# Layer norm's column sums taken from four square tiles in PSUM, and two operand splits moved beside an earlier projection

## The chip, the core and the metric

The kernel runs on one core of a Trainium2 chip. The core has five engines with queues of their own: TensorE (PE, with its weight loads shown as PEld), VectorE (DVE), ScalarE (ACT), GpSimd (POOL) and SyncE (SP), which issues DMA transfers. Each works through its own list of instructions in order and waits on semaphores for the others. The metric is the device time of one execution in microseconds (us); the median of three runs counts.

## What is computed

Two transformer-like blocks act on one sequence of 512 positions and 1024 channels, in FP32. The change touches the first block's mixer alone:

```python
def hybrid_mixer(h, w_in, b_f, conv_w, conv_b, conv_ln_g, conv_ln_b, w_o):
    proj = h @ w_in                     # q, k, v, f_logit, conv_val, conv_gate
    ...
    attn = fox_attention(q, k, v, log_f)             # 8 heads of 64, causal
    u = conv_val * jax.nn.sigmoid(conv_gate)
    u = causal_depthwise_conv(u, conv_w, conv_b)     # 512 channels, 31 taps
    u = jax.nn.silu(layer_norm(u, conv_ln_g, conv_ln_b))
    return jnp.concatenate([attn, u], axis=-1) @ w_o
```

`layer_norm` takes mean and variance over the 512 channels of a position. Behind the mixer stand a gated residual, a SwiGLU network, and the second block (a state-space mixer and a stick-breaking attention).

## The kernel before

**Tiles and precision.** The sequence is four blocks of 128 positions, the channels are blocks of 128 partitions. Projections are split products: each FP32 operand is a rounded part (hi) and its rest (lo), and `mm3` issues three matmuls (L328 hi by hi, L329, L330), each 128 rows by 512 columns, in a fast FP32 format. An ordinary FP32 matmul stands in the trace as two records, since it takes two passes.

**Where the weights come from.** SP loads weights into four raw buffers (L247). ACT rounds a raw tile (L269, `whi`) and DVE or POOL takes the rest (L273, `wlo`). Between them DVE adds up rows of other weight matrices for the modulation vectors (L503, L505).

**Layer norm over channels.** The convolution's result `yc` has channels on partitions: four tiles of 128 channels by 512 positions. A sum over channels is therefore a sum over partitions, which PE does: `colsum` (L487) multiplies a tile by a column of ones, in four pieces of 32 columns for each block of 128 positions, so that the result has one column. The steps are:

- `centre`: PE sums the total of the four tiles (L1027), DVE subtracts the mean from each (L1029);
- `square(ct)`: ACT squares tile `ct` (L1033), and POOL adds the squares, 0 to 1 and 2 to 3 (L1035) and then both sums (L1037);
- `factor`: PE takes the column sums of that one tile (16 matmuls, L487), DVE works out the inverse root in twelve small steps (L1045, L594 to L601);
- `row` and `scale`: PE spreads the factors over the partitions (L609), ACT copies them (L1052), DVE and POOL multiply (L1055), ACT applies SiLU (L1056).

**Attention.** Four pairs of heads go through projections of q and k (`main`), with evacuations that build stacked hi and lo operands (L735 and L736 for k, L738 and L739 for q); SP swaps the halves of k's stack (L750). `scores(i)` multiplies them (L756 to L761), DVE takes row maxima (L999), ACT exponentials (L1000). `attend(i)` transposes the probabilities (L777), ACT and DVE copy them (L787), PE multiplies by v (L799), spreads the reciprocals (L1012), and ACT and DVE scale the result (L1016, L1017).

**The output projection.** `Out` takes K-tiles in the order 4, 5, 6, 7, 0, 1, 2, 3: four from the convolution's side, then four from attention. `Out.split(i)` makes hi (ACT, L90) and lo (DVE, L91) of the i-th one. In `Out.steps` a split is issued when its product is about to be.

**What sets the order.** `run` mixes several lists of steps evenly into one program order. A scheduler then orders each engine's instructions by priority (the table `PRIO`, set with `prio` and `at`) and by when operands are ready. So a step that is issued earlier, or needs less, can move other instructions too. After scheduling, the order on each engine is fixed.

**The stretch around the change.** The projections of the first pair (`Q[0]`, 48 products into two PSUM tiles) run beside `centre` and `square`; pairs 1 to 3 follow beside the scores and the attention of the pair before; then come the first K-tiles of the output projection beside the last two pairs' attention.

Of the kernel before, what the change touches and what calls it, by code (L numbers as in the profile page):

```python
# [13 lines left out]
ALU = mybir.AluOpType  # L14
AX = mybir.AxisListType

P = 128
# [112 lines left out]
class Body:  # L130
# [681 lines left out]
    def fox(self):  # L812
        nc, A = self.nc, self.A
# [28 lines left out]
        for i in range(4):  # L842
# [4 lines left out]
            def ek(j, ps, i=i):  # L847
# [3 lines left out]
                for e in (0, 1):  # L851
# [7 lines left out]
        out = Out(self, A["w_o"][0], [4, 5, 6, 7, 0, 1, 2, 3],  # L859
                  lambda k: at[0][:, k, :] if k < 4 else y[0][:, k - 4, :], big=range(4))  # L860
# [128 lines left out]
        def scores(i):  # L989
            pr[i] = Ps, rs, ri = self.probs(), self.small(8), self.small(8)  # L990

            def step(t, e):
                N = (t + 1) * P
                hh = 2 * i + e
                ps = self.psum()
                self.qk(ps, X[i][:, e, :], X[i][:, 2 + e, :], Y[0][:, 2 * (i % 2) + e, :], t, self.mask_le,
                        (self.E[:, hh : hh + 1].to_broadcast([P, P]), hl))
                nm = self.small()
                nc.vector.reduce_max(nm, ps[:, :N], AX.X, negate=True)  # L999
                nc.scalar.activation(Ps[e][t], ps[:, :N], AF.Exp, bias=nm,  # L1000
                                     accum_out=rs[:, 2 * t + e : 2 * t + e + 1])
                if t == 0 and e == 1:
                    nc.vector.reciprocal(ri, rs)
            return [lambda t=t, e=e: step(t, e) for t in (3, 2, 1, 0) for e in (0, 1)]

        def attend(i, tag="pa"):
            def done(ps):

                row = self.psum()
                for t in range(NT):  # L1010
                    for e in (0, 1):
                        nc.tensor.matmul(row[64 * e : 64 * e + 64, t * P : (t + 1) * P], rhs=self.ident,  # L1012
                                         lhsT=pr[i][2][:, 2 * t + e : 2 * t + e + 1].to_broadcast([P, 64]),
                                         start=True, stop=True)
                R = self.w512()
                nc.scalar.copy(R, row)  # L1016
                nc.vector.tensor_tensor(at[0][:, i, :], ps, R, ALU.mult)  # L1017

            return self.pv(lambda: pr[i][0], v[0], i * P, done, tag)

        main = [q for i in range(1, 4) for q in Q[i]]

        box = {}
# [7 lines left out]
        def square(ct):  # L1031
            sq = box["sq", ct] = self.w512()
            nc.scalar.activation(sq, yc[:, ct, :], AF.Square)  # L1033
            if ct % 2:
                nc.gpsimd.tensor_tensor(sq, box["sq", ct - 1], sq, ALU.add)  # L1035
            if ct == 3:
                nc.gpsimd.tensor_tensor(sq, box["sq", 1], sq, ALU.add)  # L1037

        def factor():

            ps, m = self.psum(), self.small(4)
            with self.prio("colsum"):
                for t in range(NT):
                    self.colsum(ps[:, t : t + 1], [box["sq", 3][:, t * P : (t + 1) * P]])
            nc.vector.tensor_scalar(m, ps[:, 0:NT], 1.0 / 512.0, EPS, ALU.mult, ALU.add)  # L1045
            box["c"], steps = self.rsqrt(m, lambda: self.small(4))
            self.side(steps)
# [6 lines left out]
        def scale(ct):  # L1054
            (nc.vector, nc.gpsimd)[ct % 2].tensor_tensor(yc[:, ct, :], yc[:, ct, :], box["r"], ALU.mult)  # L1055
            nc.scalar.activation(yc[:, ct, :], yc[:, ct, :], AF.Silu, scale=self.v_ln_g[:, ct : ct + 1],  # L1056
                                 bias=self.v_ln_b[:, ct : ct + 1])

        idle = [lambda: None]
        sq = [lambda ct=ct: square(ct) for ct in range(4)]  # L1060

        ln = [idle + [factor], idle + [row], [lambda ct=ct: scale(ct) for ct in range(4)], [], [], []]
        self.run(Q[0][0] + Q[0][1], self.at("ln", 2 * idle + [centre] + sq) + idle)
        for i in range(3):
            self.run(main[2 * i], self.at("attend", attend(i - 1)) if i else [], self.at("ln", ln[2 * i]))
            self.run(main[2 * i + 1], self.at("scores", scores(i)) + idle, self.at("ln", ln[2 * i + 1]))
        self.run(out.steps((0, 1), (0, 1)), self.at("attend_last", attend(2, "ps")))
        self.run(out.steps((0, 1), (2, 3)), self.at("scores_last", scores(3)) + idle)
        self.run(out.steps((0, 1), (4, 5)), self.at("attend_last", attend(3, "ps")))
# [666 lines left out]
```

## Time and profile before

| | |
|---|---|
| median of 3 runs | 1370.83 us (1370.35 to 1373.17) |
| the profiled execution's own time | 1368.26 us |
| its span, first to last instruction | 1366.5 us |
| PE, matmuls | 1308.2 us busy, 96% |
| PE, weight loads | 1025.6 us, 75% |
| DVE | 855.8 us, 63% |
| ACT | 659.2 us, 48% |
| POOL | 314.1 us, 23% |
| DMA | mean 138 GB/s |

Times in the profile count from the span's start. A busy share is a mean over stages with different limits: what a change is worth is read in its own stage, from what PE waits for there. Start times of matmuls say more than their durations, since matmuls overlap and their ends are modelled.

### The profile page before, as it was taken

The numbers are of one execution on the slowest core, as the hardware profiler recorded it, in microseconds if no ns is written. First come the engines' busy times: TensorE is split into PE (matmuls) and PEld (weight loads), VectorE is DVE, ScalarE is ACT, GpSimd is POOL, SyncE is SP. The second block draws the span as 40 slices with busy tenths as digits, with TensorE's granted clock in tenths as the row PEclk, the third lists the DMA queues.
The fourth block names the chain that finished last, engine by engine and source line by source line (L and its number), as shares of the span: only waits on it lengthen the run. The fifth ranks groups of instructions, "written<-read, shape, count | busy, mean of one in ns | idle before, by whom it ended". The sixth has DMA issues, their size and how long they took to land. (4 is left out here: it accounts for less than half of the span.)

```text
span 1366.5 us, 20585 instructions
## 1 busy us (share of the span) xinstructions
PE 1308.2 (96%) x7925; PEld 1025.6 (75%) x7927; DVE 855.8 (63%) x1259; ACT 659.2 (48%) x1211; POOL 314.1 (23%) x322
## 2 busy tenths in 40 slices
PE   8899899989999999999999999999899999999997
PEld 5674666868888888888777777777688787777776
DVE  5644775463455546423878889577835956877865
ACT  5422465463322224213868475757523835555643
POOL 3542322031000000000302433333300403423421
PEclk9999999999999999999999999999999999999999
DMA  9687763024456655323258453424033364232311
GB/s 298 190 230 221 212 214 96 1 93 123 147 180 216 208 174 201 108 93 112 78 171 259 135 185 118 147 70 149 23 114 118 108 178 115 78 108 76 96 31 62
DMA packets 134734, 189.11 MB, mean 138 GB/s; under 512 B 10280, under 2 KB 95556, under 8 KB 133612
## 3 DMA queue, kind: packets, MB, share of 16 engines
q1 hardware_dynamic: 134588, 187.79, 44.9%
q8 instruction: 62, 1.02, 0.3%
q14 instruction: 36, 0.29, 0.1%
q10 hardware_dynamic: 48, 0.01, 0.0%
HBM read 178.25 MB, written 3.24 MB: 133 GB/s over the span
## 5 line engine op out<-in xcount | busy, mean ns | idle before, releaser
L273 DVE TENSOR_TENSOR wlo<-raw,whi 128x1024 fp32r<-128x1024 f32 (+1 forms) x160 | 208.4, 1314 | 210.5 <-ACT whi L269 200.4
L269 ACT CAST whi<-raw 128x1024 fp32r<-128x1024 f32 (+1 forms) x177 | 182.5, 1044 | 298.9 <-PE pa L329 128.6
L328 PE MATMUL pa<-b,whi 128*128 128x512 f32 x744 | 298.4, 401 | 0.0
L329 PE MATMUL pa<-b,whi 128*128 128x512 f32 x744 | 298.3, 401 | 0.0
L330 PE MATMUL pa<-b,wlo 128*128 128x512 f32 x744 | 297.7, 400 | 0.0
L505 DVE SCALAR_TENSOR_TENSOR acc<-raw,c,acc 128x1024 f32<-128x1024 f32 x84 | 121.4, 1446 | 81.3 <-DMA raw<-in_ada_w_dram 54.6
L328 PE MATMUL pa<-whi,b 128*128 128x512 f32 x424 | 166.3, 394 | 1.9 <-ACT b L90 1.5
L329 PE MATMUL pa<-wlo,b 128*128 128x512 f32 x424 | 166.4, 393 | 0.6 <-DVE wlo L273 0.6
L330 PE MATMUL pa<-whi,b 128*128 128x512 f32 x424 | 165.8, 393 | 0.0
L330 PEld LDWEIGHTS pa<-b,wlo 128*128 128x128 f32 x744 | 140.7, 189 | 31.9 <-issue 1.9
L328 PEld LDWEIGHTS pa<-b,whi 128*128 128x128 f32 x744 | 140.8, 189 | 31.7 <-issue 5.4
L329 PEld LDWEIGHTS pa<-b,whi 128*128 128x128 f32 x744 | 140.7, 189 | 29.5 <-issue 0.3
L681 POOL TENSOR_TENSOR b<-w,b 128x512 fp32r<-128x512 f32 x24 | 36.2, 1524 | 442.5 <-ACT b L680 389.4
L328 PEld LDWEIGHTS pa<-whi,b 128*128 128x128 f32 x424 | 79.8, 188 | 19.6 <-issue 1.8
L329 PEld LDWEIGHTS pa<-wlo,b 128*128 128x128 f32 x424 | 79.7, 188 | 17.4 <-DVE wlo L273 1.4
L330 PEld LDWEIGHTS pa<-whi,b 128*128 128x128 f32 x424 | 79.6, 188 | 17.3 <-issue 0.6
L1456 DVE TENSOR_TENSOR_SCAN w<-w,own 128x512 f32<-128x512 f32 (+3 forms) x64 | 64.1, 1046 | 15.5 <-ACT w L1453 15.5
L1458 POOL TENSOR_TENSOR w<-w,w 128x511 f32<-128x511 f32 (+3 forms) x64 | 67.7, 1063 | 21.7 <-DVE w L1456 20.8
L328 PE MATMUL ps<-whi,b 128*128 128x512 f32 x184 | 72.3, 393 | 0.0
L330 PE MATMUL ps<-whi,b 128*128 128x512 f32 x184 | 72.2, 392 | 0.0
L329 PE MATMUL ps<-wlo,b 128*128 128x512 f32 x184 | 72.1, 392 | 0.0
L777 PE MATMUL ps<-ident,w 128*128 128x128 f32 x240 | 53.2, 281 | 4.1 <-ACT w L787 3.6
(355 smaller groups left out, 2137.5 us busy)
## 6 DMA issues: line engine op xcount, KB each, us to landing
raw<-in_ada_w_dram SPq DMA_DIRECT2D x80, 512.0 KB, 4.2
raw<-in_w_ffn_in_dram SPq DMA_DIRECT2D x44, 512.0 KB, 4.6
raw<-in_m_in_w_dram SPq DMA_DIRECT2D x40, 512.0 KB, 4.0
raw<-in_w_ffn_out_dram SPq DMA_DIRECT2D x22, 512.0 KB, 3.3
b<-in_ada_w_dram SPq DMA_DIRECT2D x16, 512.0 KB, 7.9
raw<-in_kv_ada_w_dram SPq DMA_DIRECT2D x16, 512.0 KB
b<-cumd SPq DMA_DIRECT2D x8, 1024.0 KB
raw<-in_m_out_w_dram SPq DMA_DIRECT2D x16, 512.0 KB, 4.8
```

Of the source, the lines that this page charges most:

```text
L269: nc.scalar.copy(hi[:, :n], u.raw)
L273: eng.tensor_tensor(lo[:, :n], u.raw, hi[:, :n].bitcast(F32), ALU.subtract)
L328: mm(ps, lhsT=lh, rhs=rh, start=first, stop=False)
L329: mm(ps, lhsT=lh, rhs=rl, start=False, stop=False)
L330: mm(ps, lhsT=ll, rhs=rh, start=False, stop=last)
L505: nc.vector.scalar_tensor_tensor(acc, raw, ck, acc, ALU.mult, ALU.add)
L681: nc.gpsimd.tensor_tensor(lo, y[i], hi.bitcast(F32), ALU.subtract)
L777: nc.tensor.transpose(ps[:, (t - s) * P : (t - s + 1) * P], Ps()[e][t][:, s * P : (s + 1) * P], self.ident)
L1456: nc.vector.tensor_tensor_scan(R[:, 0:N][:, ::-1], R[:, 0:N][:, ::-1], self.own[:, S - N : S][:, ::-1], 0.0, ALU.mult, ALU.max)
L1458: nc.gpsimd.tensor_tensor(pr_[:, : N - 1], pr_[:, : N - 1], R[:, 1:N], ALU.mult)
```

## The change

`square` loses POOL's three additions, and `factor` gives `colsum` all four square tiles, so that PSUM adds them: 64 matmuls of one column where there were 16. The first two splits of the output projection are issued in the run of the third pair's q projection and scores; they have the same priority name as before.

```diff
         def square(ct):
             sq = box["sq", ct] = self.w512()
             nc.scalar.activation(sq, yc[:, ct, :], AF.Square)
-            if ct % 2:
-                nc.gpsimd.tensor_tensor(sq, box["sq", ct - 1], sq, ALU.add)
-            if ct == 3:
-                nc.gpsimd.tensor_tensor(sq, box["sq", 1], sq, ALU.add)
...
                 for t in range(NT):
-                    self.colsum(ps[:, t : t + 1], [box["sq", 3][:, t * P : (t + 1) * P]])
+                    self.colsum(ps[:, t : t + 1], [box["sq", ct][:, t * P : (t + 1) * P] for ct in range(4)])
...
             self.run(main[2 * i], self.at("attend", attend(i - 1)) if i else [], self.at("ln", ln[2 * i]))
-            self.run(main[2 * i + 1], self.at("scores", scores(i)) + idle, self.at("ln", ln[2 * i + 1]))
+            self.run(main[2 * i + 1], self.at("scores", scores(i)) + idle, self.at("ln", ln[2 * i + 1]),
+                     self.at("osplit", [lambda: out.split(0), lambda: out.split(1)]) if i == 2 else [])
```

PE's order around the column sums, before. `pa_1514` is the PSUM tile of the first pair's k projection, `ps_1684` that of the column sums, `w_1633` the one tile with all squares:

```order
L330 MATMUL pa_1514<-b_91,wlo_1382 128x512
L328 MATMUL pa_1514<-b_91,whi_1381 128x512
L329 MATMUL pa_1514<-b_93,whi_1381 128x512
L487 MATMUL ps_1684<-ones,w_1633 32x1 x16
L330 MATMUL pa_1514<-b_91,wlo_1382 128x512
L328 MATMUL pa_1514<-b_91,whi_1381 128x512
```

The same place now. `ps_1681` holds the sums; `w_1551`, `w_1570`, `w_1578` and `w_1632` are the squares of tiles 0 to 3:

```order
L487 MATMUL ps_1681<-ones,w_1578 32x1 x4
L328 MATMUL pa_1514<-b_91,whi_1381 128x512
L329 MATMUL pa_1514<-b_93,whi_1381 128x512
L330 MATMUL pa_1514<-b_91,wlo_1382 128x512
L487 MATMUL ps_1681<-ones,w_1632 32x1 x4
L487 MATMUL ps_1681<-ones,w_1551 32x1 x4
L487 MATMUL ps_1681<-ones,w_1570 32x1 x4
L487 MATMUL ps_1681<-ones,w_1578 32x1 x4
L487 MATMUL ps_1681<-ones,w_1632 32x1 x2
L328 MATMUL pa_1514<-b_91,whi_1381 128x512
L487 MATMUL ps_1681<-ones,w_1632 32x1
L329 MATMUL pa_1514<-b_93,whi_1381 128x512
```

Before, all sums stood in one block behind 20 products of this pair (counted from the column sums of G2, which come just ahead). Now three blocks of four stand behind the 6th, 9th and 12th product, a block of 18 behind the 15th, and from the 16th product on the scheduler has set one sum behind each product, up to the 45th; behind two of these products it is three.

ACT's order beside the third pair's scores, before. `b_1011` is `yc`, `b_2416` and `b_2523` are split operands, `b_2256` is the last pair's stack, `ps_2366` and the like are scores:

```order
L735 CAST b_2256<-pa_2175 64x512
L1000 ACTIVATE w_2285,sm_2288<-ps_2344,sm_2349 128x256
L1000 ACTIVATE w_2285,sm_2288<-ps_2355,sm_2360 128x256
L1000 ACTIVATE w_2283,sm_2288<-ps_2366,sm_2371 128x128
L787 COPY w_2407<-ps_2405 128x128
L787 COPY w_2434<-ps_2431 128x256
L787 COPY w_2407<-ps_2443 128x384
L787 COPY w_2472<-ps_2467 128x512
L269 CAST b_2409<-raw_2169 128x1024
L90 CAST b_2416<-b_1011 128x512 x2
L90 CAST b_2523<-b_1011 128x512 x2
L738 ACTIVATE b_2256<-pa_2298 64x512
```

And now, where `b_2366` is the first split operand, `b_2301` the last pair's stack and `b_2450` a weight tile:

```order
L90 CAST b_2366<-b_1011 128x512 x2
L735 CAST b_2301<-pa_2220 64x512
L1000 ACTIVATE w_2329,sm_2333<-ps_2381,sm_2386 128x384
L1000 ACTIVATE w_2330,sm_2333<-ps_2392,sm_2397 128x256
L1000 ACTIVATE w_2330,sm_2333<-ps_2403,sm_2408 128x256
L787 COPY w_2457<-ps_2455 128x128
L1000 ACTIVATE w_2328,sm_2333<-ps_2414,sm_2419 128x128
L269 CAST b_2450<-raw_2189 128x1024
L787 COPY w_2479<-ps_2476 128x256
L787 COPY w_2457<-ps_2489 128x384
L738 ACTIVATE b_2301<-pa_2343 64x512
```

The first two casts stand ahead of the second L735 now, and the weight cast L269, which stood behind all four copies L787, stands behind the first of them.

## Rows read from the trace of the kernel before

**Rows 1.** PE's waits from 130 to 262 us: total, times, longest
```profile
PE ps L487 <- POOL w L1037: 4.4, 1, 4.4
PE ps L487 <- DVE w L787: 2.0, 1, 2.0
```

**Rows 2.** Timeline of PE at the column sums: start, us, engine, line, operation [idle before]
```profile
134.81 0.39 PE L330 MATMUL pa<-b,wlo 128*128 128x512 f32 x1
...
142.79 0.61 PE L487 MATMUL ps<-ones,w 128*32 128x1 f32 x32 [4.42 <-POOL w L1037]
...
143.92 0.63 PE L328 MATMUL pa<-b,whi 128*128 128x512 f32 x1
144.35 0.63 PE L329 MATMUL pa<-b,whi 128*128 128x512 f32 x1
...
151.87 0.39 PE L328 MATMUL pa<-b,whi 128*128 128x512 f32 x1
```

**Rows 3.** Timeline of ACT and POOL: the squares and Pool's last addition
```profile
135.66 2.58 ACT L1033 ACTIVATE w<-b 128x512 f32<-128x512 f32 x4 [4.25 <-DVE b L1029]
...
140.62 2.12 POOL L1037 TENSOR_TENSOR w<-w,w 128x512 f32<-128x512 f32 x1
```

**Rows 4.** Windows: busy us of PE, PEld, DVE, ACT, POOL; granted clock; DMA
```profile
142.40:149.10 6.70, 6.31 (x46) 5.03 (x47) 4.45 (x15) 2.10 (x3) 2.71 (x2) 0.50 0.46 120
...
202.00:210.00 8.00, 8.00 (x39) 3.97 (x38) 2.10 (x4) 0.22 (x1) 0.00 (x0) 1.00 0.25 74
```

**Rows 5.** Timeline of PE: a block of column sums between products
```profile
424.89 0.39 PE L330 MATMUL pa<-b,wlo 128*128 128x512 f32 x1
425.20 0.71 PE L487 MATMUL ps<-ones,acc 128*32 128x1 f32 x64
425.85 0.50 PE L328 MATMUL pa<-b,whi 128*128 128x512 f32 x1
426.19 0.40 PE L329 MATMUL pa<-b,whi 128*128 128x512 f32 x1
```

**Rows 6.** Timeline of PE: 64-column tiles singly between products
```profile
202.59 0.50 PE L330 MATMUL pa<-b,wlo 128*128 128x512 f32 x1
203.03 0.43 PE L1012 MATMUL ps<-ident,sm 128*64 128x128 f32 x2
203.39 0.49 PE L328 MATMUL pa<-b,whi 128*128 128x512 f32 x1
```

**Rows 7.** Timeline of PE: one column sum ahead of a full tile
```profile
801.15 0.22 PE L487 MATMUL ps<-ones,acc 128*32 128x1 f32 x2
801.31 0.33 PE L1283 MATMUL ps<-ident,b 128*128 128x128 f32 x1
```

**Rows 8.** Timeline of PE: transposes, with one product between each two
```profile
341.57 0.27 PE L1089 MATMUL ps<-ident,w 128*128 128x128 f32 x1
...
341.91 0.27 PE L1089 MATMUL ps<-ident,w 128*128 128x128 f32 x1
```

**Rows 9.** Timeline of DVE and PE: from the column sums to the first scores
```profile
143.47 0.16 DVE L1045 TENSOR_SCALAR sm<-ps 128x4 f32<-128x4 f32 x1 [1.85 <-PE ps L487]
...
153.65 1.23 DVE L273 TENSOR_TENSOR wlo<-raw,whi 128x1024 fp32r<-128x1024 f32 x1 [1.97 <-ACT whi L269]
...
156.25 0.69 DVE L739 SCALAR_TENSOR_TENSOR b<-pa,b 64x512 fp32r<-64x512 f32 x1 [0.66 <-ACT b L738]
...
157.99 0.39 PE L756 MATMUL ps<-b 128*128 128x512 f32 x1
```

**Rows 10.** Timeline of PE and ACT: the first output product
```profile
225.23 0.40 PE L330 MATMUL pa<-b,wlo 128*128 128x512 f32 x1
226.85 0.50 PE L328 MATMUL pa<-b,b 128*128 128x512 f32 x1 [1.22 <-ACT b L90]
...
225.23 1.05 ACT L269 CAST b<-raw 128x1024 fp32r<-128x1024 f32 x1
226.18 2.18 ACT L90 CAST b<-b 128x512 fp32r<-128x512 f32 x4
```

## The prediction

> **What bounds the kernel now.** I read the page first: TensorE (PE) is busy 1308.2 of 1366.5 us, so only what PE waits for, or what is added to it, can move the end. Next came PE's waits in the stretch that the change touches, 130 to 262 us: the two longest are 4.4 and 2.0 us [rows 1]. The longest stands in front of layer norm's column sums (L487) and is released by Pool's last addition, L1037. Then I read the stretch in order of time. PE issues projection products 0.23 us apart, the sixth of them (after the sums of G2) at 134.81; the stall ends at 142.79; and afterwards products stand 0.43 us apart (143.92 to 144.35) instead of 0.23 [rows 2]. The granted clock says why: 0.50 from 142.4 to 149.1, that is 1.2 instead of 2.4 GHz, directly behind the idle time [rows 4]. So this wait costs some 4.6 us of standing and about 3 us of slow products (13 of them, 0.2 us too long each, and a slow block of sums). The 46th product of the stretch starts at 151.87 [rows 2]. I use this instant as the mark: all that the first edit does to PE lies before it.
>
> **The edit on the sums: what goes.** Three Pool additions go. ScalarE's four squares start at 135.66 and are done at 138.24, one each 0.63 us; Pool ends only at 142.74 [rows 3]. In the new order the first four sums stand behind the 6th product, the next behind the 9th and 12th, eighteen behind the 15th, and then single sums: one behind each product from the 16th to the 45th, twice three together. That is 30 places with a sum between two products, beside four blocks.
>
> **What comes.** 48 more sums, each two records (an FP32 product is two passes). The stream of them is cheap: 64 records take 0.65 us from their first to the next product (425.20 to 425.85) [rows 5], and two take 0.155 (801.15 to 801.31) [rows 7], so about 8 ns for each further record; 96 more would be 0.8 us. What is dear is the change between two kinds of tile, 128x128 and 128x32. Products before a block run on to its first record in 0.31 instead of 0.23, and the product behind it needs 0.34 to the next [rows 5]. Where small ones stand singly between products, the trace shows a stretch with 64-column tiles (L1012, the reciprocal rows): 0.43 us from product to small one, and 0.79 to 0.80 from product to product [rows 6]. Of this the small pair's own 128 columns are a part that a sum of one column doesn't have; a pair with one column and 32-column tiles takes 0.155 to the next full tile [rows 7]. So one place costs 0.43 + 0.155 = 0.585 us, against 0.23 of a bare product: 0.355 more.
>
> The nearest rows on both sides: a single 128x128 transpose between products, with no change of tile, makes it 0.34 from one to the next [rows 8]; the 64-column pair makes it 0.79. I take 0.585, since tile and column count are both those of a row. The Trainium skill speaks for either side. Its page TensorE: Matmul & The Clock Gate (Architectural detail) says that PE pulls weight loads ahead of running matmuls; by that alone the sums' weights would be hidden, a place would cost what the transpose shows, and PE would be 1.7 us earlier (rival A). The Trainium skill's TensorEngine Tiling (Array Packing), Key Properties, says that a change of tiling mode drains the engine. The trace agrees with the second where tiles change (0.79 and 0.585) and with the first where they don't (0.34).
>
> The Trainium skill's TensorEngine Tiling (Array Packing), Instruction Overhead, gives a matmul of one column the time of 60 cycles. At 2.4 GHz that would be 25 ns, and 2.4 us for 96 records (an estimate from that page), 1.6 more than by the rows; the trace, with 8 ns, does not agree, and the sum stays.
>
> **The sum up to the mark.** Product 6 starts at 134.81 and the first sums could follow 0.31 later, but wait for the first square, 135.66 + 0.63 + 0.05 = 136.34 (0.05 from Pool's end at 142.74 to PE's start): a wait of 1.2 us remains, a quarter of the one that the clock fell behind. A block of four sums is 8 records, 0.155 + 6 x 0.008 = 0.2; three products behind it 0.34 + 0.24 + 0.31 = 0.9. Three times that: product 16 could come at 136.34 + 3.3 = 139.6, and 36 records (18 sums) before it add 0.4: 140.0. The later squares are ready in time (138.24 at the latest). Then 30 places of 0.585: product 46 at 157.5, against 151.87. With 0.11 for the last change back, PE is **5.7 us later**. The bounds: 30 x 0.34 gives 150.2, 1.7 us earlier; 30 x 0.79 gives 163.7, 11.8 later. The wait and the slow clock do go; what they gave is spent on 30 changes of tile and more.
>
> **Who waits behind it.** The sums end at 157.5 instead of 143.4, so VectorE's next step (L1045 before, L1041 now) waits until then. Behind it in its queue stand nine small steps, one split, and the two L739 that write the first pair's queries, which the scores L756 need. A small step takes 0.16, some 0.2 with its start, so nine take 1.8; with 1.23 for the split, two L739 of 0.69 and three more small ones the second L739 ends near 162.6 [rows 9]. PE gets to the scores 5.7 us after 157.99, at 163.7. Before, that spare was 157.99 - 156.94 = 1.05, and it stays 1.1 [rows 9]. No new stall, but also nothing gained back. SyncE's queue passes one weight load over three small key copies; the copies are wanted only by those scores, many microseconds later.
>
> **The edit on the splits.** PE's first output product waits 1.22 us for a split's cast (L90), which ScalarE runs behind a 1.05 us weight cast (L269): start to start it is 226.85 - 225.23 = 1.62 instead of 0.23 [rows 10]. Now two splits stand well earlier on ScalarE and VectorE, beside the third pair's scores, where both have pauses. The number of splits is the same. The bounds are 0 and 1.4 us won. But a weight cast (1.05 us) now stands ahead of the copy L787 that the product of probabilities and values waits for, so I take 1.2: what is late next is that copy, by a few tenths. The order of the last pair's scores changes with it, without another change of tile in number.
>
> **Sum.** +5.7 - 1.2 = +4.5 us. The profiled execution took 1368.26 (span 1366.5, 1.76 around it): 1372.8. The 1368.26 lie 2.57 under the median of the runs; the same difference on the median gives 1370.83 + 4.5 = **1375.3 us**.
>
> **Rivals.**
> A. *Prefetched weights, so faster.* If the 32-column weights load under the running product, a place costs 0.34, as the transposes [rows 8]; then -1.7 - 1.2 = -2.9: 1367.9. It decides from a place under 0.43 us, where the sum is zero, and is measurable near 0.34. Against it: seven L1012 places between 202 and 210 us, all near 0.79, of which one is shown [rows 6]. 7%.
> B. *The delay is taken up later.* PE waits 2.0 us at 175.3 for VectorE's L787 [rows 1]; VectorE's modulation sums (L505), which need no PE, could get done in the 5.7 us. Against it: its queue is in order, and the sums stand behind steps that wait for PE. Then +2.5: 1373.3, no measurable change. 15%.
> C. *The second edit gives nothing*, the copy behind the weight cast stalling PE as long as the split did: +5.7, 1376.5. 12%.
> D. *The clock falls among the single sums*, since a product's own 0.23 is less than half of each 0.585 us. At half clock each product takes 0.43 instead of 0.23 [rows 2]: 30 x 0.2 = 6 more, 1381.3. For the L1012 places, busier, the clock stayed 1.00 [rows 4]. 8%.
> The forecast itself has 58%.
>
> **Numbers.** What this kernel's measurement can tell from no change is about 0.2%, 2.7 us (1368.1 to 1373.6). Slower: C, D and most of the forecast (its own range is 1373 to 1378), 72%. Same: B and the forecast's low end, 21%. Faster: A, 7%. The range from 1371 to 1380.5 leaves out A and D and a little of the rest.
>
> **What would show it.** In the changed profile: no wait of L487 for Pool; one near 1.2 us for ScalarE's first square; clock 1.00 from 140 to 150; products 0.58 us apart from about 140 to 157.5; product 46 near 157.5; DVE's L1041 then; no wait for L90 before the first output product, or one under 0.4 us. I am wrong if single sums cost under 0.45 us a place, if PE waits less at the later L787, or if the half clock shows in the new stretch.

## The result and the profile after

The changed kernel takes **1384.4 us** (median of 6 runs, 1381.6 to 1388.2) against 1370.6 of the kernel before (6 runs beside it): a ratio of 1.0098, 95% interval 1.0083 to 1.0113. It is slower, as forecast, but by 13.8 us where 4.5 were forecast, and beyond the stated range of 1371 to 1380.5. The profiled execution took 1384.85 us (span 1383.0).

The page of the changed kernel, PE's busy time and the granted clock in 40 slices of the span:

```profile
PE 1329.2 (96%) x8021; PEld 1036.0 (75%) x8023; DVE 856.0 (62%) x1259; ACT 659.7 (48%) x1211; POOL 306.6 (22%) x319
...
PEclk9999699999999999999999999999999999999999
```

PE is busy 21 us longer than before, for 96 more records of 8021. The fifth slice (138 to 173 us) stands at 6: there the clock was low. PE's waits in the stretch that answers to [rows 1], 130 to 280 us:

```profile
PE ps L487 <- DVE w L787: 2.0, 1, 2.0
PE ps L777 <- ACT w L1000: 1.7, 3, 0.9
PE ps L487 <- ACT w L1033: 1.1, 1, 1.1
```

The wait of 4.4 for Pool is gone and so is the one for L90; 1.1 for the first square has come, and the waits of L777 for ScalarE's exponentials (L1000) are 1.7 together, 0.2 before. None of it makes a kernel slower by 14 us. The timeline of PE at the column sums, against [rows 2], shows where the time went:

```profile
137.50 0.24 PE L487 MATMUL ps<-ones,w 128*32 128x1 f32 x8 [1.14 <-ACT w L1033]
...
140.70 0.48 PE L487 MATMUL ps<-ones,w 128*32 128x1 f32 x36
141.11 0.50 PE L328 MATMUL pa<-b,whi 128*128 128x512 f32 x1
141.54 0.22 PE L487 MATMUL ps<-ones,w 128*32 128x1 f32 x2
141.69 0.50 PE L329 MATMUL pa<-b,whi 128*128 128x512 f32 x1
...
145.94 0.79 PE L330 MATMUL pa<-b,wlo 128*128 128x512 f32 x1
146.67 0.27 PE L487 MATMUL ps<-ones,w 128*32 128x1 f32 x2
146.86 0.79 PE L328 MATMUL pa<-b,whi 128*128 128x512 f32 x1
...
166.21 0.79 PE L328 MATMUL pa<-b,whi 128*128 128x512 f32 x1
166.80 0.63 PE L329 MATMUL pa<-b,whi 128*128 128x512 f32 x1
...
169.32 0.39 PE L329 MATMUL pa<-b,whi 128*128 128x512 f32 x1
169.55 0.39 PE L330 MATMUL pa<-b,wlo 128*128 128x512 f32 x1
...
173.88 0.39 PE L756 MATMUL ps<-b 128*128 128x512 f32 x1
```

One sum between two products: first 0.58 us from product to product (141.11 to 141.69), then 0.92 (145.94 to 146.86). The 46th product comes at 166.21. The windows show the clock that goes with it (busy us of PE, PEld, DVE, ACT, POOL; granted clock; DMA share, GB/s):

```profile
141.20:145.30 4.10, 4.10 (x22) 2.31 (x22) 1.32 (x2) 0.00 (x0) 0.00 (x0) 1.00 0.68 238
145.40:166.20 20.80, 20.80 (x77) 10.50 (x76) 3.66 (x3) 2.11 (x3) 2.36 (x1) 0.50 0.35 102
```

The clock fell to 0.50 (1.2 GHz) seven places into the alternation, and from then on PE was busy 20.80 of 20.80 us: it never stood idle. It came back only behind plain products, which are 0.43 apart at 166.80 and 0.23 at 169.32.

So that runs can be laid over each other, times below count from the first product of the stretch (133.54 before, 134.69 after), read from the timelines. The scores' line is L760 in e9 to e13; the last mark is the output projection's first product with a weight tile as its left operand (`pa<-whi,b`). The times are those of one profiled execution each, the medians those of all runs:

| kernel | 46th product | first scores L756 | output's first streamed product | median us | ratio to before (95%) |
|---|---|---|---|---|---|
| before | 18.3 | 24.4 | 119.8 | | |
| changed | 31.5 | 39.2 | 134.8 | 1384.4 | 1.0098 (1.0083 to 1.0113) |
| e1 one block | 14.2 | 20.3 | 120.0 | 1374.3 | 1.0016 (1.0000 to 1.0032) |
| e2 splits only | 17.4 | 23.5 | 119.7 | 1372.9 | 1.0006 (0.9994 to 1.0018) |
| e3 sums only | 32.2 | 40.6 | 135.2 | 1388.9 | 1.0123 (1.0104 to 1.0142) |
| e5 full tiles, fp32 | 40.8 | 48.4 | 143.9 | 1401.5 | 1.0210 (1.0186 to 1.0233) |
| e6 filler products | 25.1 | 40.0 | 135.1 | 1388.0 | 1.0110 (1.0082 to 1.0138) |
| e8 full tiles, fp32r | 27.8 | 36.4 | 132.1 | 1384.6 | 1.0078 (1.0049 to 1.0108) |
| e9 block, reads left out | 13.9 | 20.1 | 114.9 | 1367.3 | 0.9960 (0.9942 to 0.9978) |
| e11 block, maxima first | 13.9 | 20.0 | 116.9 | 1369.2 | 0.9977 (0.9964 to 0.9991) |
| e12 before, maxima first | 17.9 | 24.0 | 121.9 | 1374.3 | 1.0019 (1.0006 to 1.0033) |
| e13 as e11, no split edit | 13.9 | 20.0 | 117.7 | 1368.1 | 0.9978 (0.9965 to 0.9991) |

Runs of before beside the experiments had medians of 1371.7 to 1371.8. The loss stands complete at the first scores: 39.19 - 24.45 = 14.74 us. Behind them nothing of it is given back: at the last mark it is 15.0.

### The profile page after: what moved, and what is told of

It reads as the page before. It is cut to its first block, busy times and chain, and to the rows that moved or that the text cites. A ratio compares the mean times of both kernels' runs of the same rounds, so it can differ in the third digit from the quotient of the medians.

```text
span 1383.0 us, 20768 instructions
## 1 busy us (share of the span) xinstructions
PE 1329.2 (96%) x8021; PEld 1036.0 (75%) x8023; DVE 856.0 (62%) x1259; ACT 659.7 (48%) x1211; POOL 306.6 (22%) x319
## 3 DMA queue, kind: packets, MB, share of 16 engines
q8 instruction: 63, 1.03, 0.3%
## 5 line engine op out<-in xcount | busy, mean ns | idle before, releaser
L269 ACT CAST whi<-raw 128x1024 fp32r<-128x1024 f32 (+1 forms) x177 | 182.6, 1045 | 313.4 <-PE pa L329 142.2
L328 PE MATMUL pa<-b,whi 128*128 128x512 f32 x744 | 302.0, 406 | 0.0
L329 PE MATMUL pa<-b,whi 128*128 128x512 f32 x744 | 301.2, 405 | 0.0
L505 DVE SCALAR_TENSOR_TENSOR acc<-raw,c,acc 128x1024 f32<-128x1024 f32 x84 | 120.9, 1439 | 76.0 <-DMA raw<-in_ada_w_dram 51.7
L330 PEld LDWEIGHTS pa<-whi,b 128*128 128x128 f32 x424 | 79.8, 188 | 17.4 <-issue 0.8
L273 POOL TENSOR_TENSOR wlo<-raw,whi 128x1024 fp32r<-128x1024 f32 (+1 forms) x17 | 41.7, 2460 | 90.8 <-ACT whi L269 68.0
```

Source lines behind the costliest of these rows:

```text
L269: nc.scalar.copy(hi[:, :n], u.raw)
L273: eng.tensor_tensor(lo[:, :n], u.raw, hi[:, :n].bitcast(F32), ALU.subtract)
L328: mm(ps, lhsT=lh, rhs=rh, start=first, stop=False)
L329: mm(ps, lhsT=lh, rhs=rl, start=False, stop=False)
L330: mm(ps, lhsT=ll, rhs=rh, start=False, stop=last)
L505: nc.vector.scalar_tensor_tensor(acc, raw, ck, acc, ALU.mult, ALU.add)
```

## The experiments

**What was to be told apart.** Theory T: the loss is the change of tile at each single sum and the half clock that the stretch brought. Against it: the sums are dear by themselves (R1), the wait for the first square pulled the clock down (R2), the splits carry a part (R3).

**e1, one block.** The sums of layer norm's `factor` get the priority of the convolution's products:

```diff
-            with self.prio("colsum"):
+            with self.prio("conv_mm"):
```

> The changed kernel with one thing different: the column sums of the squares get the priority of the convolution's products, so that after the last square the remaining 48 stand in one block instead of one between every two products. The same 64 sums, no Pool additions, both edits in. Theory T (the loss is the tile change of each single sum, 0.355 us at full clock, and the half clock that the thin alternating stretch brought): product 46 comes 46 x 0.213 + 1.14 (wait for the first square) + 4 short blocks x 0.4 + one long block of about 0.8 = 13.3 us after product 1, against 18.3 before and 31.5 in the changed kernel; granted clock 1.00 throughout; some 5 us below before, 1365.6. Rival R1 (the 48 added sums cost their 0.3 to 0.6 us each wherever they stand): about as the changed kernel, 1384. Rival R2 (the 1.1 us wait for the first square is what lowers the clock): half clock again, 1372 to 1376.

Timeline of PE in this kernel: after three blocks of four, the other 52 sums stand in one block, 104 records (the expectation said 48).

```profile
141.80 1.04 PE L487 MATMUL ps<-ones,w 128*32 128x1 f32 x104
142.77 0.50 PE L328 MATMUL pa<-b,whi 128*128 128x512 f32 x1
```

0.97 us for 104 records: R1 falls; the sums cost 9 ns a record, and what was dear is where they stood. The 46th product comes 4.1 us sooner than before. (R2 is not decided here: by chance a slow stretch lay over the first six products and the wait for the square vanished in it. e6 and e11 decide it: both have the wait, of 1.13 us, and clock 1.00 behind it, e11 from 136 to 153 us.) But the kernel is not 5 us faster; the 4.1 are gone again by the output's first streamed product. That part of the expectation was wrong. PE's waits from 153 to 178 us, and VectorE's timeline ahead of the first row maximum (L999):

```profile
PE ps L756 <- ACT w L1000: 2.2, 2, 1.2
```

```profile
157.34 3.10 DVE L505 SCALAR_TENSOR_TENSOR acc<-raw,c,acc 128x1024 f32<-128x1024 f32 x1 [2.55 <-DMA raw<-in_ada_w_dram]
160.36 0.74 DVE L503 TENSOR_SCALAR acc<-raw,c 128x1024 f32<-128x1024 f32 x1
161.14 0.69 DVE L999 TENSOR_REDUCE sm<-ps 128x1 f32<-128x512 f32 x1
```

PE waits for exponentials, these for the row maxima, and the maxima stand in VectorE's order behind a modulation sum (L505) whose weights had not come. In before PE came 4 us later and VectorE did not wait there. But these waits are only 2.2 of the 4.4 us by which the way from the first scores to the last mark is longer than before (99.7 against 95.3). Another 1.7 is the clock. PE waits 2.0 us for VectorE's L787 in both kernels, and the half clock behind this wait lasts longer here. The windows around it in before, e1, e2 and e12, and in e3, where the wait comes later:

```profile
174.00:188.00 14.00, 12.69 (x137) 9.04 (x137) 10.23 (x16) 7.61 (x13) 0.02 (x1) 0.88 0.77 259
174.00:188.00 14.00, 11.75 (x126) 8.77 (x127) 10.12 (x16) 6.30 (x12) 0.00 (x0) 0.76 0.64 211
174.00:188.00 14.00, 12.71 (x130) 9.51 (x131) 9.22 (x14) 6.45 (x11) 0.00 (x0) 0.76 0.73 228
174.00:188.00 14.00, 10.68 (x122) 7.65 (x122) 9.11 (x14) 8.88 (x16) 0.00 (x0) 0.76 0.71 235
188.00:200.00 12.00, 9.58 (x129) 6.74 (x128) 10.68 (x15) 7.19 (x14) 0.50 (x1) 1.00 0.67 227
```

The granted clock is 0.88 in before and 0.76 in e1, and 0.12 of 14 us is 1.7. e2 and e12 have 0.76 too, without the waits of L756, and in e3 the clock does not fall behind that wait at all. So this share is not shown to come from VectorE's order; it differs between executions with the same wait. The waits themselves were taken further in e9 to e13.

**e2 and e3, each edit alone.** e2 is the kernel before with the splits edit, e3 with the sums edit.

```diff
-            self.run(main[2 * i + 1], self.at("scores", scores(i)) + idle, self.at("ln", ln[2 * i + 1]))
+            self.run(main[2 * i + 1], self.at("scores", scores(i)) + idle, self.at("ln", ln[2 * i + 1]),
+                     self.at("osplit", [lambda: out.split(0), lambda: out.split(1)]) if i == 2 else [])
```

```diff
-            if ct % 2:
-                nc.gpsimd.tensor_tensor(sq, box["sq", ct - 1], sq, ALU.add)
-            if ct == 3:
-                nc.gpsimd.tensor_tensor(sq, box["sq", 1], sq, ALU.add)
...
-                    self.colsum(ps[:, t : t + 1], [box["sq", 3][:, t * P : (t + 1) * P]])
+                    self.colsum(ps[:, t : t + 1], [box["sq", ct][:, t * P : (t + 1) * P] for ct in range(4)])
```

> The kernel before with only the second edit: the output's first two K-tiles are split beside the third pair; Pool's additions stay. The forecast on record has -1.2 us for it: 1369.4. The trace of the changed kernel says that the 1.2 us wait is gone but its time is not (95.6 us from the first scores to the output's first streamed product, 95.3 before): 1370.6 within 0.5. Rival R3 (the splits, not the sums, carry a part of the loss, through ScalarE): 1373 or more.

> The kernel before with only the first edit: 64 sums over the four squares, no Pool additions, the order of the splits as before. Theory T: all of the loss is here, 1384 to 1385, with half clock in the alternating stretch and a cycle of 0.92 us in it. Rival R3 (a part of the loss is the splits'): at least 2 us below the changed kernel, 1382 or less.

e3 has the whole loss, and R3 falls. It is 4.5 us above the changed kernel, which was not expected; in its trace the clock fell already five places into the alternation (near 143.6 us) and came back later, which is the 1.4 us between them at the first scores, and by the last mark 0.4 is left. The two intervals overlap, so what remains is not told apart from the scatter of runs. e2 gives nothing, and lies 2.3 us above what was expected, with the kernel before beside it at 1371.7: the interval excludes the 1.2 us only just (0.9994 is 0.8 us), but the trace says why it is none. PE's waits in e2, and ScalarE's timeline ahead of the last exponentials of the third pair:

```profile
PE ps L777 <- ACT w L1000: 1.2, 3, 0.6
```

```profile
219.80 1.14 ACT L90 CAST b<-b 128x512 fp32r<-128x512 f32 x2
220.97 0.58 ACT L735 CAST b<-pa 64x512 fp32r<-64x512 f32 x1
221.58 0.58 ACT L1000 ACTIVATE w<-ps,sm 128x384 f32<-128x384 f32 x1
```

The split's two casts now stand ahead of an exponential, which PE's transposes L777 wait for: those waits grow from 0.2 to 1.2 us in the same stretch, nearly what L90 had cost.

**e5, e8 and e6: tile and clock apart.** e5 and e8 keep number and order of PE's instructions in the stretch and take the change of tile away: each small product covers a full 128x128 tile, in fp32 (e5) or fp32r (e8, two columns). e6 keeps the small tiles and adds idle products.

The line of `colsum` in `factor` becomes, in e5, e8 and e6 in this order (the main lines of each edit; in e8 the squares change their type too):

```diff
+                    for ct in range(4):
+                        for j in range(4):
+                            nc.tensor.matmul(ps[:, t : t + 1], lhsT=box["sq", ct][:, t * P : (t + 1) * P],
+                                             rhs=self.ones[:, 0:1], start=ct + j == 0, stop=ct + j == 6)
```

```diff
+            sq = box["sq", ct] = self.w512(F32R)
...
+                            nc.tensor.matmul(ps[:, 2 * t : 2 * t + 2], lhsT=box["sq", ct][:, t * P : (t + 1) * P],
+                                             rhs=one, start=ct + j == 0, stop=ct + j == 6)
```

```diff
+                    for ct in range(4):
+                        for j in range(0, P, 32):
+                            nc.tensor.matmul(ps[j : j + 32, t : t + 1], lhsT=box["sq", ct][:, t * P + j : t * P + j + 32],
+                                             rhs=self.ones[:, 0:1], start=ct == 0, stop=ct == 3)
+                            if 16 * t + 4 * ct + j // 32 >= 18:
+                                nc.tensor.matmul(spare[:, 0:496], lhsT=h[1][0][:, 0, 0:P], rhs=h[0][0][:, 0, 0:496],
+                                                 start=True, stop=True)
```

> The changed kernel with the same 64 small products in the same places, one between every two of the projection's, but each over a whole 128x128 tile (out 128x1) instead of a 128x32 one; each square's sum is added four times and the factor 1/512 is 1/2048. Nothing changes in number, order or waits; only the tile of the small products is that of their neighbours. Theory T: without a change of tile a place costs its own 2 records of 8 ns and perhaps a weight load that is not quite hidden, 0.02 to 0.1 us in place of 0.355; the stretch keeps full clock; product 46 comes 12 to 17 us after product 1 (31.5 in the changed kernel); 1364 to 1370. Rival R1 (any product of one column between two of 512 columns costs it): 1384. Rival R2 (the wait for the first square lowers the clock): half clock from about 145 us on and 1372 or more.

e5 was expected to be fast and is the slowest of all. Its timeline, the first block at full clock and a place at half clock:

```profile
139.13 1.05 PE L1042 MATMUL ps<-ones,w 128*128 128x1 f32 x8 [1.14 <-ACT w L1033]
140.04 0.48 PE L328 MATMUL pa<-b,whi 128*128 128x512 f32 x1
...
151.53 0.77 PE L330 MATMUL pa<-b,wlo 128*128 128x512 f32 x1
152.11 0.42 PE L1042 MATMUL ps<-ones,w 128*128 128x1 f32 x2
152.39 0.77 PE L328 MATMUL pa<-b,whi 128*128 128x512 f32 x1
```

A full-tile record of one column takes 0.91 / 8 = 0.114 us in this first block, 0.81 / 8 = 0.101 in the next, against 0.009 of a 32-column one. What differs is the tile of weights, 128 columns against 32, which is loaded for each record. So this edit took the change of tile away and put two loads in its place (0.85 - 0.43 = 0.42 a place at half clock, 0.92 - 0.43 = 0.49 with the small tile). The test was confounded, and T's "0.02 to 0.1" was wrong for fp32. The Trainium skill's TensorE: Matmul & The Clock Gate, LDWEIGHTS (loading the stationary operand), says that a weight load's time goes by its columns; 0.101 to 0.114 against 0.009 has that direction.

> As the full-tile kernel, same 64 places, but the squares and the ones are fp32r, so each small product is one record with one weight load (out 128x2, two columns): the tile and type of its neighbours. The full-tile fp32 kernel showed 0.85 a cycle at half clock against 0.92 of the small tiles, so its 0.02 to 0.1 was wrong; two readings are left. Theory T (change of tile): without it a place costs one weight load that a product of one column can't hide, up to 0.12 at full clock: a cycle of 0.23 to 0.35, full clock from 141 to the 46th product, which comes 12 to 16 us after product 1; with the give-back that the one-block kernel shows, 1368 to 1375. Rival L (any short product between two long ones costs the same 0.355, whatever its tile and type): a cycle of 0.58, then half clock, 1384 to 1390.

```profile
144.63 0.48 PE L328 MATMUL pa<-b,whi 128*128 128x512 f32 x1
144.95 0.17 PE L1042 MATMUL ps<-one_r,w 128*128 128x2 f32 x1
144.97 0.53 PE L329 MATMUL pa<-b,whi 128*128 128x512 f32 x1
...
146.65 0.78 PE L329 MATMUL pa<-b,whi 128*128 128x512 f32 x1
147.23 0.20 PE L1042 MATMUL ps<-one_r,w 128*128 128x2 f32 x1
147.29 0.78 PE L330 MATMUL pa<-b,wlo 128*128 128x512 f32 x1
```

With one load and no change of tile the cycle is 0.34 at full clock (144.63 to 144.97, the only one there) and 0.64 at half, so a place costs 0.11 and 0.21 where the small tile costs 0.355 and 0.49. e5's two loads in the other number format cost 0.42 at half clock, twice the 0.21, so the change of format from fp32r to fp32 adds nothing that shows. That settles the price: most of it is the change of tile. The Trainium skill's TensorEngine Tiling (Array Packing), Key Properties, says that such a change drains the engine, and the pair of kernels agrees. Rival L falls by the price of a place, though the time is the one it forecast. For the clock fell in e8 too, at about 145.3, and T had expected it to hold. It fell two products behind the block of 18 full-tile sums (142.70 to 144.63), so e8 does not show that single sums alone bring the fall; it shows that the clock falls, and stays at half through all single sums, without any change of tile.

> The changed kernel with work added: 46 idle products (full tile, 496 columns, into a PSUM tile that nobody reads) are queued between the column sums, so that three full products instead of one stand between two single sums. Theory C (the clock fell because the stretch was thin in streamed columns, not because of the small products): granted clock 1.00 in the whole stretch; from one sum to the next 0.355 + 2 x 0.213 + 0.207 = 0.99 us; in all 46 x 0.207 = 9.5 of idle products and some 42 places of 0.355 = 14.9, less the 4.4 of Pool's wait and the half clock of before behind it (some 6): 1388 to 1392. Rival R4 (each small product or change of tile lowers the clock by itself): half clock here too, about 16 us more, 1403 or above.

```profile
142.71 0.22 PE L1042 MATMUL ps<-ones,w 128*32 128x1 f32 x2
142.86 0.50 PE L328 MATMUL pa<-b,whi 128*128 128x512 f32 x1
143.19 0.39 PE L1045 MATMUL ps<-b,b 128*128 128x496 f32 x1
143.42 0.40 PE L329 MATMUL pa<-b,whi 128*128 128x512 f32 x1
143.74 0.22 PE L1042 MATMUL ps<-ones,w 128*32 128x1 f32 x2
```

```profile
141.00:173.00 32.00, 32.00 (x157) 18.99 (x157) 12.22 (x12) 4.35 (x6) 2.38 (x1) 1.00 0.60 178
```

With three long products to a sum the clock is 1.00 in all 32 us, with the same small tiles and the same wait of 1.13 for the first square ahead of it; one cycle is 1.03 us (0.99 expected). R2 and R4 fall. So, of the three kernels, those with one long product to a sum lost the clock, with a change of tile (changed) and without (e8); the one with a change of tile and three long products to a sum (e6) kept it. Whether the streaming kept it, or the sums standing further apart (1.03 us instead of 0.58), these runs do not tell: the fillers do both at once. e6 has done 38 of its 46 fillers of 496 columns by the first scores and reaches them only 0.8 us later than the changed kernel: what these cost, the clock gave back, nearly.

**e9 to e13: where the block's gain went.** e9 is e1 with four reads of modulation weights replaced by zeros. e11 is e1 with four modulation sums bound to start behind row maxima; e12 is the kernel before with that order alone; e13 is e11 without the splits edit.

In the loads (e9) and in the modulation sums (e11):

```diff
...
+                if isinstance(u, Sums) and 16 <= self.nada <= 19:
+                    self.nc.gpsimd.memset(u.raw, 0.0)
...
```

```diff
...
+                if 16 <= self.nsum <= 19:
+                    n = (0, 0, 1, 3)[self.nsum - 16]
+                    self.wait(op.ins, self.maxima[n].ins)
...
```

> The one-block kernel with four reads left out: the four chunks of the modulation weights (512 KB each) that VectorE sums just ahead of the first row maxima are set to zero by Pool instead of read from memory, so the modulation they belong to is wrong. Theory W (the 4 us that the block gained before the scores went to VectorE's in-order wait of 2.55 us for one of these reads, behind which the row maxima stand): the two waits of PE for ScalarE's exponentials (0.97 and 1.19) go, the way from the first scores to the output's first product is 68.9 to 70 us instead of 73.6, about 3.5 below the one-block kernel: 1370 to 1371. Rival V (VectorE's and ScalarE's own work sets the scores' pace): the waits stay, 1374 as the one-block kernel.

> The one-block kernel with VectorE's order changed at one place: four of the modulation sums (L505, L503) may start only after the first, first, second and fourth row maximum of the first pair, so that no row maximum stands behind a read of weights that has not come. Nothing is left out. Theory W (the block's 4 us went to that in-order wait): PE's waits for ScalarE's exponentials between 160 and 168 us go, the way from the first scores to the output's first product falls from 73.6 to 69 to 70 us, and the kernel comes to 1367 to 1369.5, below before. Rival X (the weights are then late for the projection's own splits, so the stall moves to PE's products): waits for whi or wlo in their place, 1372 to 1375.

> The kernel before, both edits left out, with the same change of VectorE's order alone. VectorE waits for no read of weights there in that stretch of before, so theory W expects nothing: 1371.7 within 1.5. If this order is worth something by itself, it shows here: 1369 or less, and then the gain of the one-block kernel with it is not the sums'.

> The one-block kernel with the row maxima first, without the second edit (the output's splits stay where they were). The splits alone measured +0.06% (between -0.06 and +0.18), so: the same as with them within 1.5 us, 1367 to 1370.5. If the splits beside the third pair cost something when PE runs ahead, this is 2 us or more below its sister.

In e9 PE's waits of L756 for the exponentials are gone, and it is 7 us below e1, twice what was expected: PE's 2.0 us wait for VectorE's copy, behind which e1 has its half clock, is gone from its trace too, so by itself it shows the direction, not the size. In e11 nothing is left out. PE's timeline at the first square, VectorE's at the maxima (L1003 here), PE's waits from 153 to 180 us:

```profile
136.17 0.24 PE L487 MATMUL ps<-ones,w 128*32 128x1 f32 x8 [1.13 <-ACT w L1038]
```

```profile
154.40 0.69 DVE L1003 TENSOR_REDUCE sm<-ps 128x1 f32<-128x512 f32 x1 [2.06 <-PE ps L765]
...
155.83 2.17 DVE L505 SCALAR_TENSOR_TENSOR acc<-raw,c,acc 128x1024 f32<-128x1024 f32 x1
```

```profile
PE ps L487 <- DVE w L791: 2.2, 1, 2.2
PE ps L781 <- ACT w L791: 0.6, 1, 0.6
PE ps L781 <- ACT w L1004: 0.5, 1, 0.5
```

The maximum now waits for PE and not for memory, the two waits of L756 are gone, the way from the first scores to the output's first product is 70.5 us (73.6 in e1; 69 to 70 expected), and the kernel is at 0.9977 of before: **faster by 2.5 us, the first that beats both with nothing left out**. Theory W holds for the waits, X falls. For the whole 4 us W is too much: from the first scores to the last mark e11 is 2.8 us shorter than e1, the waits of 2.2 and a shorter half clock (0.88 in the same window) among it, while waits of L781 for exponentials grew. The order is not the gain itself: on the kernel before (e12) it costs 0.19%, 2.6 us where 1.5 were allowed for. With that order in both, the block of sums (with the splits edit, which is worth nothing) gives 1374.3 - 1369.2 = 5 us, as e1 was meant to show; 4.0 of it stand at the first scores, and 3.4 of these are the half clock behind Pool's wait, which e12 has (0.62 from 141 to 150 us) and e11 has not. e13 has the same ratio as e11, so the splits edit is worth nothing here either.

## Why the prediction was wrong, step by step

- **Waits (right).** No wait for Pool, 1.14 us for the first square (1.2 forecast). Three blocks and the long one stood where they were said to; the 16th product came 6.4 us after the first, 6.5 forecast.
- **Price of a place (right).** "So one place costs 0.43 + 0.155 = 0.585 us": 0.43 + 0.15 = 0.58 measured while the clock was full (141.11, 141.54, 141.69), both halves as forecast, and e8 shows that the change of tile is most of it.
- **Clock in the new stretch (the step that failed).** The forecast had "clock 1.00 from 140 to 150; products 0.58 us apart from about 140 to 157.5". The clock fell at about 145.4, seven places in. From the 16th to the 46th product PE took 25.1 us where 30 x 0.58 = 17.4 was the sum: 7.7 us; the products from the 46th until the clock came back lost 1.4 more. 5.7 + 7.7 + 1.4 = 14.8, the 14.74 seen at the first scores. This is rival D, which had 8%. It was held down by the window of L1012 places in [rows 4], clock 1.00. But those seven places are not one run. A block of other products stands between the fourth and the fifth (`205.66 1.67 PE L799 MATMUL pa<-w,b 128*64 128x256 f32 x11`). So there are four places up to 204.97 and three from 207.26 on, neither run longer than the seven that kept full clock here, and each place has 128 columns of its own. PE's full busy share there says nothing, since it was as full here at half clock. D's size was wrong too: it counted only the products' own 0.2 us a place, while the change slows as well (0.355 to 0.49), 0.34 together.
- **Who waits behind (right).** The first pair's queries were no new stall, and the 2.0 us in front of the later L487 stayed 2.0: rival B took nothing up.
- **The splits (wrong).** The wait for L90 went, as said, but the 1.2 us came back as waits of L777 for exponentials that now stand behind the split's casts. The working had named the copy L787 as next and a few tenths as its price; it was the exponentials, and 1.0 in e2, 1.5 here. That is rival C's price, paid at another instruction than the copy that C named.

With both corrections the forecast's own sum gives 1375.3 + 1.2 + 9.1 = 1385.6, against 1384.4. That they meet within 1.2 us is partly luck: 9.1 is read from one execution, and in e3, with the same order of PE in the stretch, the clock fell two places sooner.

Open: why the clock falls where it does. The runs show what PE did before it fell, and that more long products between the sums kept it up, not which of their effects counts. The 0.19% of e12 stands in its trace: 97.9 us from the first scores to the last mark against 95.3, with 1.1 more of waits in all and the longer half clock, 1.7; why the waits grew was not followed.

## What to carry to other kernels

Trading additions on an idle engine for more matrix products is cheap only if the products stand together: ask the order, not the count, for the price. Small products of another tile shape, put singly between long ones, paid a change of tile each time, and the clock went to half among them although PE never stood idle: a busy PE does not show it. Read the granted clock of such a stretch, and where no row of the kernel has so long an unbroken run of such places, give half clock a real chance. A gain on PE is safe only when the in-order queues behind it can use it: here about half of the 4 us gained went to waits behind one vector instruction that waited for weights, and another order took these waits away. And look at the granted clock of both traces before a difference of 2 us is put down to a wait.

## What the runs showed that was not expected

- The clock fell to half although PE was busy 20.80 of 20.80 us. The Trainium skill's TensorE: Matmul & The Clock Gate, HAM oscillation — how this bites in real kernels, ties the fall to idle gaps; in this stretch there was none, and with 46 further products (e6) the clock stayed up.
- A full-tile product of one column takes 0.101 to 0.114 us a record in fp32 where a 128x32 one takes 0.009, so 16 sums over full tiles, in one block, would take 3.2 to 3.6 us (32 records) and 64 over small ones 128 x 0.009 = 1.2 (an estimate from e5 and e1).
- Behind a wait of 2.0 to 2.3 us for the same copy, half clock cost 1.7 us in before, 3.4 in e1, e2 and e12, and nothing in e3 (estimates: 0.12 and 0.24 of 14 us of granted clock).
- In e1 the modulation sum that waited 2.55 us for its read took 3.10 when it ran, where the next one of its size took 1.28; why was not followed.
